# A two-layer hybrid trunk on one core: the build's scheduler with another simulated machine

## The chip, the cores and the metric

One Trainium2 chip, one of its cores. The metric is the device time of one execution in microseconds (us). The kernel is built with the Tile layer of the Bass language: the Python program traces instructions, a scheduler in the build orders them, and the result is one fixed instruction stream for each engine.

## The reference

The reference computes two layers of a diffusion trunk over 1024 latent tokens and a prompt of 128 tokens, 1024 channels wide, in 32-bit floats. Each layer is

```python
h = rms_norm(x, P['g_pre_mix']) * (1.0 + sc1) + sh1
o, extra = mixer(h)
x = x + gt1 * rms_norm(o, P['g_post_mix'])
h = rms_norm(x, P['g_pre_mlp']) * (1.0 + sc2) + sh2
m = einsum(square(relu(einsum(h, P['mlp_w1']))), P['mlp_w2'])
x = x + gt2 * rms_norm(m, P['g_post_mlp'])
```

where the scales, shifts and gates come from a conditioning vector times `w_ada`. The mixer is one input projection (`w_in`) that feeds four groups of heads: latent attention (MLA), banded attention with a sink (SWA), a gated delta rule that runs forward and backward over the tokens in chunks of 64 (GDN), and a long convolution of order 2 (Hyena). Their outputs are concatenated and multiplied by `w_out`. Beside the two token streams the kernel returns the prompt's keys, values and final GDN states.

## The kernel before

`Trunk.build` traces two layers one after the other. All 1152 tokens (9 tiles of 128) are handled together. Each wide product is split in two halves of precision: an operand x becomes `hi` (rounded) and `lo` (the rest, made at L232), and `mm3` (L215 to L219) multiplies hi by hi, hi by lo and lo by hi. So a weight tile is loaded by DMA into a staging buffer of the pool `T`, which has 4 buffers (L251 in `load_cols`, L241 in `load_rows`), cast on ScalarE (ACT) and subtracted on VectorE (DVE) before TensorE (PE) can use it.

A layer has these stages, in the order of the trace:

- the normed and transposed input, and 22 tiles of the input projection (`pj`), traced by a generator `rest` (L2098) that goes on to the Hyena convolutions and the six attention heads;
- beside it a generator `other` (L2108) with the GDN: two preparations (`gdn_prep`, L1083) and a scan of 16 serial steps (`gdn_scan`), all of it traced with a priority raised by 300 (L2121);
- a third generator `adas` (L2092) that loads `w_ada` in 192 pieces of 256 KB in all and multiplies them (`ada`, L385 to L396);
- the output projection (`out_proj`, L1744) with the second norm;
- the MLP (`mlp`, L1776): 15 blocks and a last one (`mlp_last`), each with two column tiles of `w1` (hidden, PSUM tiles `hid`) and two row tiles of `w2` (output, PSUM tiles `mo`), summed into SBUF tiles `acc`.

`run_timed` (L2190) weaves the three generators by hand-given weights, so the trace order is already an interleaving. All DMAs, loads and stores alike, are issued by one engine, SyncE (SP), in one queue. In a few places `issue_after` pins a DMA behind another one on SP.

One place matters below. In `gdn_prep` a 32 by 32 triangular inverse `N` is built in 31 serial steps, for the forward direction on DVE and for the backward direction on GpSimd (POOL) (L1195 to L1204). Then, for each direction, ACT makes a transposed copy `Tb` and SP stores both:

```python
for dr in range(2):
    Tb = W("Tb", (32, 32))
    nc.scalar.copy(out=Tb[:72], in_=N[dr][:72]...)      # L1209
    nc.sync.dma_start(out=nscr[dr, 0]..., in_=N[dr]...)  # L1210
    nc.sync.dma_start(out=nscr[dr, 1]..., in_=Tb...)     # L1211
```

They are read back in another layout (`NT` L1221, `NaTG` L1224), and the products `G` follow on PE. The other place is the attention's row of maxima: ACT writes `mrow` (L719), SP stores it (L720) and reads it back.

What the scheduler does with the trace, by the library's own description: each engine has a heap of instructions by priority, which is the place in the traced program (with the raise above). It runs a simulated machine; when an engine is free there, the instruction of the highest priority whose inputs are finished and whose tile has a free slot in its pool is taken next. The order in which instructions are taken is the order of the engine's stream on the chip, and the slot that was free is the buffer. Waits on semaphores are then added for what the streams need of one another. [...] `TileContext` at L2229 has a flag for which simulated machine is used.

## Time and profile before

| | us |
|---|---|
| median of 3 runs | 3828.64 |
| fastest and slowest of them | 3820.32 and 3840.5 |
| the profiled execution | 3820.2 |
| its span, first to last instruction | 3818.4 |
| TensorE busy in it | 3535.5 |
[...]

The times are of whole executions. The rows below come from the profiled one, whose own time is 8.4 us under the median and 1.8 us over its span. Busy time of PE is the union of its matmuls; a stretch that runs at the lower clock counts as busy for longer. In a timeline the number in brackets is how long the engine sat idle before the instruction, and what released it.

### The profile page before, as it was taken

The page shows a single profiled execution, that of the slowest core. Times are in us where ns is not written, and L with a number is a line of the kernel's source. Part 1 is how long each engine was busy: PE and PEld are TensorE (multiplying, and loading weights), DVE is VectorE, ACT ScalarE, POOL GpSimd, SP SyncE. Part 2 cuts the span into 40 slices and gives each one's busy share as a digit, 9 for nine tenths or more (in the row PEclk, how much of TensorE's full clock was granted, in tenths as well). Part 3 has the DMA queues.
Part 4 walks back from the last instruction along what each step waited for, and adds up shares of the span by engine and source line. Part 5 has one row for each costly group of instructions (what it writes and reads, how often), then busy time and mean ns, then how long its engine had stood idle before and what let it go on. Part 6 is the DMA issues. An engine that isn't in the chain of part 4 may idle for free. (4 is left out here: it accounts for less than half of the span.)

```text
span 3818.4 us, 57318 instructions
## 1 busy us (share of the span) xinstructions
PE 3535.5 (93%) x21674; PEld 2988.0 (78%) x21674; DVE 2278.2 (60%) x4583; ACT 1349.5 (35%) x2930; POOL 857.7 (22%) x806
## 2 busy tenths in 40 slices
PE   7989888799999999999989888877999999999998
PEld 4879774376789999999878887545767899999997
DVE  5765567697645444444586673677884544444446
ACT  5434343265543112212364334323554422222112
POOL 1152531164420000000131642213553200000003
PEclk9999889897999999999999898896889999999999
DMA  5346476832421111111324455765314211111113
GB/s 203 115 118 159 135 261 205 242 80 59 148 80 50 39 45 45 41 37 45 109 100 137 121 138 164 251 208 139 96 40 139 72 45 45 44 45 45 39 39 121
DMA packets 364670, 405.29 MB, mean 106 GB/s; under 512 B 115815, under 2 KB 237157, under 8 KB 364394
## 3 DMA queue, kind: packets, MB, share of 16 engines
q1 hardware_dynamic: 364394, 401.63, 34.2%
q8 instruction: 170, 2.79, 0.3%
q14 instruction: 106, 0.87, 0.1%
HBM read 298.34 MB, written 103.19 MB: 105 GB/s over the span
## 5 line engine op out<-in xcount | busy, mean ns | idle before, releaser
L213 PE MATMUL hid<-hT,w1h 128*128 128x384 f32 x3072 | 786.6, 335 | 0.1
L213 PE MATMUL pj<-hT,wah 128*128 128x384 f32 x2112 | 574.4, 350 | 8.9 <-ACT hu L1740 3.9
L1823 DVE TENSOR_TENSOR acc<-acc,mo 128x512 f32<-128x512 f32 x504 | 345.9, 686 | 391.9 <-PE mo L213 391.9
L213 PEld LDWEIGHTS hid<-hT,w1h 128*128 128x128 f32 x3072 | 557.7, 188 | 14.4 <-ACT h L481 1.1
L213 PE MATMUL hid<-hT,w1l 128*128 128x384 f32 x1536 | 514.2, 335 | 0.0
L213 PE MATMUL mo<-w2h,ul 128*128 128x512 f32 x1116 | 435.2, 392 | 0.0
L213 PE MATMUL mo<-w2h,uh 128*128 128x512 f32 x1080 | 422.8, 391 | 0.0
L213 PE MATMUL mo<-w2l,uh 128*128 128x512 f32 x1080 | 422.6, 391 | 0.0
L213 PEld LDWEIGHTS pj<-hT,wah 128*128 128x128 f32 x2112 | 395.0, 196 | 21.9 <-issue 6.0
L662 POOL TENSOR_TENSOR e<-e,e 128x512 f32<-128x512 f32 (+1 forms) x216 | 312.9, 1450 | 298.0 <-ACT e L651 141.6
L269 POOL TENSOR_TENSOR postr<-postr,mhalf 128x1 f32<-128x1 f32 x36 | 22.4, 623 | 1570.4 <-DVE postr L268 1569.1
L213 PE MATMUL pj<-hT,wal 128*128 128x384 f32 x1056 | 367.2, 348 | 0.0
L242 ACT CAST w2h<-w 128x512 fp32r<-128x512 f32 x128 | 70.3, 619 | 732.9 <-PE mo L213 728.8
L213 PEld LDWEIGHTS hid<-hT,w1l 128*128 128x128 f32 x1536 | 288.2, 188 | 2.5
L232 DVE TENSOR_TENSOR el<-e,eh 128x512 fp32r<-128x512 f32 (+1 forms) x252 | 252.4, 1023 | 33.8 <-ACT eh L653 31.9
L213 PEld LDWEIGHTS mo<-w2h,ul 128*128 128x128 f32 x1116 | 209.7, 188 | 46.2
L213 PEld LDWEIGHTS mo<-w2h,uh 128*128 128x128 f32 x1080 | 202.8, 188 | 37.5
L213 PEld LDWEIGHTS mo<-w2l,uh 128*128 128x128 f32 x1080 | 202.7, 188 | 36.5
L213 PEld LDWEIGHTS pj<-hT,wal 128*128 128x128 f32 x1056 | 205.8, 195 | 3.7 <-issue 2.0
L1806 DVE SCALAR_TENSOR_TENSOR relu<-hid,relu 128x384 f32<-128x384 f32 x180 | 99.4, 553 | 166.8 <-ACT relu L1805 166.8
L213 PE MATMUL ada<-wada,cst 128*32 128x512 f32 x384 | 138.2, 683 | 31.3 <-DMA wada<-in_w_ada 31.0
L1805 ACT ACTIVATE relu<-hid 128x384 f32<-128x384 f32 x180 | 87.9, 488 | 184.4 <-PE hid L213 184.4
(498 smaller groups left out, 6360.2 us busy)
## 6 DMA issues: line engine op xcount, KB each, us to landing
w<-in_w SPq DMA_DIRECT2D x256, 256.0 KB
wada<-in_w_ada SPq DMA_DIRECT2D x192, 256.0 KB
wa<-in_wa SPq DMA_DIRECT2D x88, 256.0 KB
x<-xres SPq DMA_DIRECT2D x21, 512.0 KB
x<-in_x SPq DMA_DIRECT2D x18, 512.0 KB
Q<-rscr SPq DMA_DIRECT2D x32, 288.0 KB
o<-oscr SPq DMA_DIRECT2D x18, 512.0 KB
xres<-x SPq DMA_DIRECT2D x36, 256.0 KB
```

The lines of the kernel that those rows point to most:

```text
L213: self.last = self.nc.tensor.matmul(out, l, r, start=start, stop=stop, skip_group_check=True)
L232: self.nc.vector.tensor_tensor(out=lo, in0=x, in1=hi.bitcast(F32), op=ALU.subtract)
L242: self.nc.scalar.copy(out=hi[:, q], in_=st)
L269: self.nc.gpsimd.tensor_tensor(out=out, in0=out, in1=self.bcs(self.mhalf[:out.shape[0]], out.shape), op=ALU.pow)
L662: self.nc.gpsimd.tensor_tensor(out=acc, in0=acc, in1=e, op=ALU.add)
L1805: nc.scalar.activation(out=r[:, :n], in_=ps[:, :n], func=AF.Relu)
L1806: nc.vector.scalar_tensor_tensor(out=r[:, :n], in0=ps[:, :n], scalar=0.0, in1=r[:, :n], op0=ALU.max, op1=ALU.mult)
L1823: nc.vector.tensor_tensor(out=acc[t][:, ns], in0=acc[t][:, ns], in1=ps, op=ALU.add)
```

## The change

The build's scheduler gets its other simulated machine: it runs against the library's core simulator in place of its timeline simulator. The traced program, its priorities, the pools and the operations stay as they are; what can differ is each engine's order, the buffer that a tile gets, and the waits that follow from both.

```diff
-    with tile.TileContext(nc, schedule_with_timeline_sim=True) as tc:
+    with tile.TileContext(nc, schedule_with_timeline_sim=False) as tc:
         Trunk(tc, I, O).build()
```

## Rows read from the trace of the kernel before

**Rows 1.** The page's first lines: span, and PE's busy time and instructions.
```profile
span 3818.4 us, 57318 instructions
PE 3535.5 (93%) x21674; PEld 2988.0 (78%) x21674; DVE 2278.2 (60%) x4583; ACT 1349.5 (35%) x2930; POOL 857.7 (22%) x806
```
**Rows 2.** Stretches: start:end length, busy by engine (count), clock, DMA share, GB/s.
```profile
0.00:42.00 42.00, 29.20 (x96) 8.75 (x96) 18.68 (x39) 14.00 (x29) 2.92 (x8) 1.00 0.84 304
42.00:1000.00 958.00, 850.99 (x6249) 673.07 (x6247) 658.94 (x1511) 426.42 (x954) 349.90 (x326) 0.89 0.50 148
1000.00:1113.00 113.00, 110.18 (x512) 88.97 (x511) 51.46 (x104) 52.19 (x110) 32.10 (x34) 1.00 0.42 138
1113.00:1905.00 792.00, 791.84 (x4023) 720.96 (x4024) 394.96 (x649) 184.30 (x377) 25.85 (x25) 1.00 0.16 52
1905.00:1968.00 63.00, 46.62 (x249) 37.71 (x248) 49.23 (x97) 43.53 (x100) 31.68 (x29) 0.86 0.27 92
1968.00:2895.00 927.00, 802.98 (x6026) 649.23 (x6025) 652.93 (x1429) 397.67 (x890) 341.81 (x317) 0.88 0.47 141
2895.00:3038.00 143.00, 138.50 (x658) 113.96 (x658) 62.85 (x134) 59.40 (x129) 38.76 (x40) 1.00 0.34 116
3038.00:3806.00 768.00, 765.16 (x3873) 695.36 (x3871) 383.69 (x622) 172.00 (x348) 26.17 (x23) 1.00 0.16 52
3806.00:3818.40 12.40, 0.00 (x0) 0.00 (x0) 5.52 (x6) 0.00 (x0) 8.53 (x7) 0.54 0.34 128
```
**Rows 3.** The same view, three stretches inside the second layer's mixer.
```profile
1968.00:2200.00 232.00, 214.44 (x1728) 197.20 (x1728) 153.55 (x332) 97.79 (x181) 74.02 (x82) 0.95 0.45 133
2200.00:2422.00 222.00, 186.01 (x1983) 174.19 (x1982) 134.65 (x326) 89.07 (x231) 73.90 (x89) 0.91 0.54 155
2422.00:2605.00 183.00, 143.54 (x1173) 82.48 (x1172) 135.21 (x411) 51.55 (x170) 37.13 (x38) 0.84 0.73 235
```
**Rows 4.** Timeline of PE, 262 to 300 us: start, length, instruction [idle before].
```profile
265.41 1.14 PE L229 MATMUL ht<-ident,hc 128*128 128x128 f32 x9
284.85 0.70 PE L213 MATMUL G<-NaTG,Q 32*32 32x32 f32 x8 [18.30 <-DMA NaTG<-nscr]
285.48 1.01 PE L213 MATMUL pj<-hT,wah 128*128 128x384 f32 x2
...
293.77 0.33 PE L213 MATMUL pj<-hT,wal 128*128 128x384 f32 x1
```
**Rows 5.** Timeline of ACT, 262 to 292 us.
```profile
281.38 1.95 ACT L1209 COPY Tb<-N 72x1024 f32<-72x1024 f32 x1 [15.39 <-POOL N L1204]
283.23 0.61 ACT L253 CAST wah<-wa 128x512 fp32r<-128x512 f32 x1
283.75 0.47 ACT L518 COPY hcx<-pj 128x384 f32<-128x384 f32 x1
```
**Rows 6.** Timeline of POOL, 262 to 284 us: the last step of N.
```profile
281.08 0.27 POOL L1204 TENSOR_TENSOR N<-N,tmp 72x31 f32<-72x31 f32 x1
```
**Rows 7.** Timeline of SP's DMA issues, 255 to 300 us.
```profile
264.65 0.31 SPq L1211 DMA_DIRECT2D nscr<-Tb  x1
281.37 0.29 SPq L1210 DMA_DIRECT2D nscr<-N  x1
...
291.38 1.18 SPq L251 DMA_DIRECT2D wa<-in_wa  x2
```
**Rows 8.** Waits of PE over the whole span: us in total, times, longest.
```profile
PE ada L213 <- DMA wada<-in_w_ada: 31.0, 24, 5.9
PE G L213 <- DMA NaTG<-nscr: 31.0, 9, 18.3
...
PE ST L213 <- DMA Q<-mscr: 9.9, 1, 9.9
```
**Rows 9.** Waits of SP's DMA queue over the whole span, same columns.
```profile
SPq L251 <- DVE w2l L232: 784.3, 59, 27.3
...
SPq L720 <- ACT mrow L719: 178.1, 14, 40.3
```

## The prediction, as it was put on record

> **What bounds the kernel now.** I read the page's head first: TensorE is busy for 3535.5 of 3818.4 us, 93%, and no other engine is over 60% [rows 1]. That would say "TensorE-bound, nothing to win or lose by order", but it is an average, so I cut the span into stages [rows 2]. The reader is to see two kinds. The two MLP stretches (1113 to 1905 and 3038 to 3806) are 1560 us long and TensorE is busy in 1557.0 of them, at the full clock of 2.4 GHz. The two output projections (113 and 143 us) have 248.7 of 256 busy. The mixers and the passage between the layers (42 to 1000, 1905 to 1968, 1968 to 2895) are 1948 us long, and there TensorE is busy for 851.0 + 46.6 + 803.0 = 1700.6 us, 87.3%, at a mean granted clock of 0.86 to 0.89, which means that it spends part of that time at the lower level of 1.2 GHz. 247.4 us of idle TensorE lie in these stretches, against 3 us in the MLP. Start and end (42 and 12.4 us) complete the span.
>
> So the change can act on about half of the span. What ends the idle stretches there is read from TensorE's waits: they are many and small, spread over some 60 pairs of waiter and releaser; the largest two sums are 31.0 us each [rows 8]. There is no single stall whose removal or growth is the answer; the question is how well four streams of work (projection and attention, GDN, Hyena, conditioning) fill one another's gaps.
>
> **What one misjudged place costs.** The longest wait of all, 18.3 us, shows what an order can do [rows 4 to 7]. POOL finishes the last step of the backward inverse N at 281.3. ACT's stream has the copy `Tb`, which needs this N, ahead of the cast of the next projection weight and ahead of the copy that empties a projection's PSUM tile, so ACT sits idle for 15.4 us and those two run at 283.2 and 283.8. SP's stream has the store of the same N ahead of the next weight loads, so between 265.0 and 281.4 it issues nothing, and the weights are issued at 291.4. TensorE, whose projection needs the weight and the PSUM tile, and whose `G` needs N, sits from 266.5 to 284.9. When it starts again, two matmuls take 1.01 us together, where the same pair took 0.51 before the gap, until the clock is back some 6 us later. The simulated machine let the copy go first because in its time N was ready; on the chip it was not. One such error, in two queues at once, costs 18.3 us of idle and about 3 us of slow matmuls.
>
> **The change part by part.** There is one edit with three effects.
>
> (1) Removed and added work: none. The same matmuls, copies and DMAs are issued. Cost 0; TensorE's busy time at the full clock can't change.
>
> (2) The MLP and the output projections: the order there follows from buffers and data. SP spends 784.3 us in 59 waits, about 13 us each, for staging or weight buffers to come free [rows 9], so the loads run ahead of TensorE as far as the buffers go under any order that respects the trace. I take 0. What covers it is one block of matmuls, 1560/32 = 49 us for each of the 32 blocks; were the cover gone and each block paid one load wait like the longest single one of an attention tile, 9.9 us [rows 8], it would be 317 us. With 3 us of idle time in 1560 nothing can be gained there.
>
> (3) The mixers: every engine's order is drawn again, from other durations and other landing times. The trace of before shows neither, so I bound it by stretches of the kernel that show the same kind of work at a better and a worse fill [rows 3]. If all 1700.6 us of busy time were filled as 1968 to 2200 is (214.44/232 = 92.4%), the mixers would take 1840 us, 108 less. If all were filled as 2422 to 2605 is (143.54/183 = 78.4%), they would take 2168, 220 more. Filled as the GDN preparation beside the projection of the second layer (2200 to 2422, 186.01/222 = 83.8%): 2030, which is 82 more. As a scale for what one order differs from another: the first layer's mixer has 851.0/958 = 88.8% and the second's 803.0/927 = 86.6%, with nearly the same work; over 1948 us these two shares are 49 us apart.
>
> I take the middle one, +82 us, nearest to the row of 2200 to 2422. The reason is where the idle time comes from. It is made where an in-order queue holds an instruction whose input comes later than the simulation had it (the 18.3 us above). A machine that follows queues, contention and durations less closely has more of these, and 82 us are four places of 18.3 + 3 us more, in two layers with two GDN preparations, two convolutions and six heads each. An order that by luck removes the present ones gains at most their sum. The row against me is the same one: the present machine, too, misjudged POOL, so it isn't exact either.
>
> Sum: 3820.2 (the profiled execution) + 0 + 0 + 82 = 3902; the median of the runs is 8.4 us above that execution, so 3910.
>
> **A rule weighed.** The row: from 266.5 to 284.9 TensorE sat still with projection matmuls behind `G` in its stream, and `G` went first when it came [rows 4]. [...]
>
> **The rivals.**
>
> *Faster.* The new order no longer puts the backward `Tb` and its store ahead of weights in ACT's and SP's streams. Place: the four GDN preparations. For it: the 31.0 us that TensorE waits for `NaTG` [rows 8], 18.3 of them in one wait, are errors of the present order; the work to fill them was there. Price: with the `NaTG` waits and as much again from the conditioning loads (31.0) gone, 62 us, so 3767 from the median; at most the 108 us of the bound, 3720. It decides from the point where POOL's last step is simulated to end after the projection's next weight is ready. Against it: these are 62 of 247 us, and the other 185 us are drawn again too.
>
> *No change.* Data dependences and few buffers (4 staging buffers) fix the order so far that both machines come to nearly the same streams; or the flag has no effect. 3829, within 19. For it: the MLP is such a case. Against it: in the mixers four streams with work ready at the same time compete for each queue.
>
> *Much slower.* SP stops at a store while loads that TensorE needs stand behind it. Place: the attention's store of `mrow`: SP already sits 178.1 us in 14 waits for it, up to 40.3 each, and only 9.9 us of that reaches TensorE [rows 8, 9], because what stands behind is not needed yet. Price with this cover gone: 168 us more, 3997. It decides from the point where a load needed within 40 us is queued behind such a store.
>
> **How the numbers follow.** A difference of 0.5%, 19 us, is about what a measurement of this kernel can tell from none. Chances: the forecast (slower by 20 to 150 us) 0.51, much slower (150 to 260) 0.18, no change 0.13, faster 0.18. Faster 0.18, same 0.13, slower 0.69. The range: the upper end is the bound of 220 us, 4040 from the profiled execution, above which I leave a third of the much slower case, 0.06. The lower end is 3780, which leaves the better part of the faster case, 0.10. That is 0.16 outside. The forecast's own range is 3848 to 3979.
>
> **What would show it.** In the profile after: TensorE still 99% busy or more in both MLP stretches, so that they keep 1560 us (if not, step 2 is wrong); TensorE's idle time in the mixers about 330 us in place of 247 and their clock at or under 0.88 (step 3); new waits of 5 us or more of TensorE on a load or on ACT, with SP or ACT idle before a store or copy that needs POOL, DVE or ACT (the mechanism). If the idle time grows without such long waits, spread over many small ones, the size may be right and the mechanism is wrong. If the wait for `NaTG` goes and nothing takes its place, the faster rival holds. If the streams are the same, nothing changes.

## The result, and the profile after

| | before | after |
|---|---|---|
| median of 4 runs each, taken side by side, us | 3826.47 | 4146.99 |
| ratio of the times, 95% interval | | 1.083 [1.081, 1.086] |
| the profiled execution, us | 3820.2 | 4145.76 |
| TensorE busy in it, us | 3535.5 | 3753.4 |
| mean granted clock of TensorE | 0.941 | 0.902 |

The change makes the kernel 8.3% slower. The forecast was 3910 with a range of 3780 to 4040: the direction was right, and the time lies 107 us above the range.

The page's first lines of after (answers to [rows 1]):

```profile
span 4144.0 us, 57252 instructions
PE 3753.4 (91%) x21674; PEld 3091.4 (75%) x21674; DVE 2314.4 (56%) x4583; ACT 1360.2 (33%) x2930; POOL 837.0 (20%) x806
```

The instructions are the same, 21674 matmuls in both. The reader is to see that the busy time of TensorE grew by 217.9 us with equal matmuls, and its idle time (span less busy) by 107.7, from 282.9 to 390.6. The sum is the 325.6 us that the span grew.

Not all of the added busy time comes from the clock. The traces tell the granted clock at every moment: TensorE is busy at the full clock (1.00) for 3209.9 us in before and 3117.9 in after, and at the lower level, half of it (0.50), for 325.6 and 635.5. If work takes twice as long at half the clock, an estimate from the pair of matmuls that the prediction names (1.01 us right behind the 18.3 us gap, at 0.50, against 0.51 before it, at 1.00; the next pairs at 0.50 take 0.84), the clock accounts for half of the 309.9 us more, 155 us; the other 63 of the 217.9 us are busy time that it does not explain by this estimate.

Where they lie. I cut both spans at the same events of TensorE: the first and last matmul of the input projection `pj`, the first transpose `hoT` of the convolutions' output (the attention takes over), the first matmul of the output projection, the first of the MLP.

| stage, us | layer 0 before | after | layer 1 before | after |
|---|---|---|---|---|
| up to the projection | 42.0 | 56.5 | | |
| projection, with GDN preparation | 495.8 | 572.9 | 490.8 | 611.8 |
| convolutions | 161.1 | 170.3 | 175.7 | 169.5 |
| attention | 303.1 | 371.1 | 288.7 | 336.2 |
| output projection | 111.7 | 105.7 | 116.7 | 114.9 |
| MLP, to the next projection or the end | 817.3 | 815.7 | 815.5 | 819.4 |

Projection (+198) and attention (+116) hold nearly all of it; another 14.5 us lie ahead of the first projection. The same cuts as stretches of the trace (start:end length, then busy time and count of PE, PEld, DVE, ACT and POOL, PE's clock, DMA share, GB/s), before:

```profile
42.00:538.00 496.00, 441.07 (x3840) 404.03 (x3838) 308.54 (x738) 220.23 (x478) 161.42 (x183) 0.91 0.49 141
538.00:699.00 161.00, 130.29 (x1211) 75.59 (x1209) 123.32 (x385) 49.05 (x172) 34.21 (x37) 0.87 0.76 243
699.00:1002.00 303.00, 281.20 (x1207) 194.10 (x1205) 228.38 (x392) 158.69 (x306) 156.19 (x108) 0.87 0.40 108
1931.00:2422.00 491.00, 428.81 (x3869) 395.06 (x3869) 312.16 (x703) 209.02 (x461) 161.83 (x183) 0.92 0.48 139
2422.00:2597.00 175.00, 137.56 (x1144) 76.89 (x1143) 128.31 (x387) 49.04 (x165) 37.13 (x38) 0.85 0.73 236
2597.00:2886.00 289.00, 255.97 (x1139) 193.90 (x1139) 230.75 (x376) 158.46 (x307) 156.65 (x108) 0.84 0.30 80
```

and after (the last two are the MLPs):

```profile
56.00:629.00 573.00, 497.28 (x4649) 438.73 (x4650) 343.76 (x907) 251.70 (x615) 156.82 (x179) 0.89 0.41 121
629.00:800.00 171.00, 116.20 (x403) 59.74 (x402) 107.09 (x235) 9.25 (x13) 36.58 (x38) 0.80 0.73 235
800.00:1171.00 371.00, 339.34 (x1214) 220.30 (x1213) 235.33 (x366) 163.63 (x311) 149.06 (x108) 0.78 0.28 76
2092.00:2704.00 612.00, 531.27 (x4669) 459.41 (x4670) 347.98 (x893) 258.10 (x624) 165.42 (x187) 0.84 0.41 119
2704.00:2873.00 169.00, 109.82 (x397) 58.69 (x396) 105.35 (x234) 9.58 (x18) 36.37 (x37) 0.82 0.72 230
2873.00:3210.00 337.00, 309.82 (x1150) 215.07 (x1149) 228.39 (x363) 162.59 (x310) 150.05 (x108) 0.78 0.23 60
...
1276.00:2068.00 792.00, 785.54 (x3993) 715.70 (x3993) 398.54 (x652) 188.30 (x382) 28.05 (x28) 1.00 0.16 52
...
3324.00:4092.00 768.00, 767.28 (x3913) 699.81 (x3914) 381.16 (x618) 175.15 (x348) 15.85 (x16) 1.00 0.15 48
```

Three things are to be seen. About 800 matmuls moved from the convolutions (1211 to 403) into the projection (3840 to 4649), and the convolutions did not get shorter for it (some 20 us of each are now one wait, named below). The attention has the same matmuls (1207 and 1214) and is 93% busy before and 91% after, yet it takes 68 us longer, at a clock of 0.78 in place of 0.87. The MLPs are as they were.

The moved matmuls are the GDN scan's. The matmuls that write or read a tile `u` of the scan, in the first two stretches of layer 0, before:

```profile
42.00:538.00 496.00, 11.00 (x320) 8.80 (x320) 8.87 (x52) 9.23 (x34) 0.91 0.49 141
538.00:699.00 161.00, 26.85 (x832) 21.47 (x832) 30.62 (x164) 30.32 (x110) 0.87 0.76 243
```

and after:

```profile
56.00:629.00 573.00, 51.53 (x1152) 38.54 (x1152) 39.26 (x216) 37.15 (x144) 0.89 0.41 121
629.00:800.00 171.00, 0.00 (x0) 0.00 (x0) 0.00 (x0) 0.00 (x0) 0.80 0.73 235
```

All 1152 run inside the projection now, where 832 ran beside the convolutions.

The waits that the prediction's mechanism is about (us in total, times, longest; answers to [rows 8, 9]). TensorE's of after:

```profile
PE G L213 <- DMA NaTG<-nscr: 33.3, 9, 18.7
PE O L213 <- DVE el L232: 27.6, 63, 2.1
PE pj L213 <- ACT wah L253: 26.9, 4, 13.2
...
PE oT L229 <- DVE gsk L276: 20.7, 1, 20.7
PE oT L229 <- DVE gsr L277: 19.9, 1, 19.9
```

SP's, after and then before:

```profile
SPq L1210 <- POOL N L1204: 87.8, 4, 27.3
```

```profile
SPq L1210 <- POOL N L1204: 18.3, 2, 16.3
```

ACT's, after and then before:

```profile
ACT e L651 <- PE ST L213: 197.7, 86, 37.2
```

```profile
ACT e L651 <- PE ST L213: 68.1, 38, 16.2
```

SP stands before POOL's `N` in all four GDN preparations now, 87.8 us against 18.3, but TensorE's wait for `NaTG` is about what it was (31.0). The two longest waits of after are new: once in each layer, in the convolutions, TensorE stands some 20 us before the transposes `oT` of the scan's output. The wait for the cast weight `wah` has no counterpart in before either. In all, TensorE idles for 5 us or longer 10 times in before (85.7 us) and 16 times in after (153.1 us), which is 67.4 of the 107.7 us of idle time added. In the attention ACT's exponentials `e` wait for the scores tile `ST` three times as long.

### The profile page after: what moved, and what is told of

Read it like the earlier page. It is cut to its first block, busy times and chain, and to the rows that moved or that the text cites. A ratio compares the mean times of both kernels' runs of the same rounds, so it can differ in the third digit from the quotient of the medians.

```text
span 4144.0 us, 57252 instructions
## 1 busy us (share of the span) xinstructions
PE 3753.4 (91%) x21674; PEld 3091.4 (75%) x21674; DVE 2314.4 (56%) x4583; ACT 1360.2 (33%) x2930; POOL 837.0 (20%) x806
## 3 DMA queue, kind: packets, MB, share of 16 engines
q1 hardware_dynamic: 364394, 401.63, 31.4%
## 5 line engine op out<-in xcount | busy, mean ns | idle before, releaser
L213 PE MATMUL pj<-hT,wah 128*128 128x384 f32 x2112 | 598.3, 360 | 37.7 <-ACT wah L253 26.9
L662 POOL TENSOR_TENSOR e<-e,e 128x512 f32<-128x512 f32 (+1 forms) x216 | 299.1, 1385 | 493.1 <-ACT e L651 315.0
L213 PE MATMUL pj<-hT,wal 128*128 128x384 f32 x1056 | 380.4, 361 | 6.7 <-DVE wal L232 6.7
L269 POOL TENSOR_TENSOR postr<-postr,mhalf 128x1 f32<-128x1 f32 x36 | 19.9, 554 | 1597.0 <-DVE postr L268 1589.8
L651 ACT ACTIVATE e<-ST 128x512 f32<-128x512 f32 x162 | 96.3, 597 | 237.9 <-PE ST L213 197.7
```

Of the source, the lines that this page charges most:

```text
L213: self.last = self.nc.tensor.matmul(out, l, r, start=start, stop=stop, skip_group_check=True)
L269: self.nc.gpsimd.tensor_tensor(out=out, in0=out, in1=self.bcs(self.mhalf[:out.shape[0]], out.shape), op=ALU.pow)
L651: nc.scalar.activation(out=e[:, :n], in_=ps[:, :n], func=AF.Exp, scale=scale)
L662: self.nc.gpsimd.tensor_tensor(out=acc, in0=acc, in1=e, op=ALU.add)
```

## Experiments

All kernels below are the same traced program unless a diff says otherwise. Most fix an engine's order with edges that add no wait: the program is built once with the other flag, its order is taken, and the second build must keep that order for chosen engines and for instructions traced in chosen stages. The diffs are shortened.

```diff
+def pinned(order, engines):
+    place = {n: k for k, n in enumerate(order)}
+    def pin(tc, line):
+        for e, stages in engines.items():
+            mine = [i for k, i in enumerate(line) if str(i.engine).endswith(e) and i.name in place and stage(k) in stages]
+            mine.sort(key=lambda i: place[i.name])
+            for a, b in zip(mine, mine[1:]):
+                tc.add_manual_dep(b, a.name, NoSync, reason="order of the other schedule")
...
-    with tile.TileContext(nc, schedule_with_timeline_sim=True) as tc:
+    with tile.TileContext(nc, schedule_with_timeline_sim=False) as tc:
         Trunk(tc, I, O).build()
+        pin(tc, nc.cur_bb.bb.instructions)
...
+    order_of_before = order_of(arrays, True)
```

"Front" is what is traced from the start of a layer's mixer (in the first layer from the start of the program) to its attention, "attention" what is traced from there to the output projection, "rest" the output projection and the MLP.

| run | build | pinned or edited | median, us | ratio to before, 95% |
|---|---|---|---|---|
| e1 | after | all engines to before's order | 3836 | 1.001 [0.998, 1.003] |
| e2 | after | TensorE | 4074 | 1.064 [1.060, 1.067] |
| e3 | after | front: all | 3986 | 1.040 [1.037, 1.044] |
| e4 | after | attention: all | 4061 | 1.061 [1.058, 1.064] |
| e5 | after | front: all; attention: TensorE | 3901 | 1.018 [1.014, 1.022] |
| e6 | after | front: all; attention: all but TensorE | 3969 | 1.035 [1.031, 1.040] |
| e7 | after | attention: all; front: SP | 4031 | 1.052 [1.048, 1.056] |
| e8 | after | attention: all; front: TensorE, SP | 3975 | 1.037 [1.033, 1.041] |
| e9 | after | scan traced late | 4092 | 1.070 [1.065, 1.074] |
| e10 | after | split scores tiles joined | 4140 | 1.082 [1.079, 1.086] |
| e11 | after | e9 and e10 | 4089 | 1.068 [1.064, 1.072] |
| e12 | after | `Tb` and `N` stores on POOL | 4139 | 1.082 [1.078, 1.085] |
| e13 | after | scores raised by 40 | 4118 | 1.074 [1.070, 1.079] |
| e14 | after | e9 and e13 | 4065 | 1.062 [1.057, 1.067] |
| e15 | before | attention: TensorE to after's order | 3967 | 1.035 [1.030, 1.039] |
| e16 | before | scores raised by 40 | 3863 | 1.008 [1.006, 1.011] |
| e17 | after | front: all; attention: scores and O on TensorE | 3913 | 1.022 [1.018, 1.026] |
| e18 | after | all engines to after's order, 168 matmuls more | 4131 | 1.078 [1.075, 1.081] |

### Is it the order alone?

```diff
+        pin = pinned(order_of_before, {e: ("front", "attention", "rest") for e in ("PE", "SP", "Activation", "DVE", "Pool")})
```

> The build of after, with every engine's instruction order pinned to the order of before (edges that fix only the order in a stream, no waits). What stays of after is what its simulated machine does beside the order: which free buffer a tile gets, and the waits that follow. Theory 'order alone': 3827 us, within 15 of before. Rival 'buffers': the buffers were handed out by a machine with other durations, so waits for slots stay; some 3900 or more.

Measured: 3836 us, ratio 1.001. The page's head:

```profile
span 3828.3 us, 57317 instructions
PE 3542.6 (93%) x21674; PEld 2993.3 (78%) x21674; DVE 2278.9 (60%) x4583; ACT 1353.0 (35%) x2930; POOL 856.6 (22%) x806
```

Busy and idle time of TensorE are back within 8 us. Order alone carries the loss; the buffers that the other machine hands out cost nothing that can be measured.

### Which stage

```diff
+        pin = pinned(order_of_before, {e: ("front",) for e in ("PE", "SP", "Activation", "DVE", "Pool")})
```

> The build of after with all engines pinned to before's order only for what is traced before a layer's attention (projection, GDN, Hyena convolutions, and the conditioning beside them). By the stage marks of the two traces the attention stages are longer by 72 + 47.5 = 120 us in after, the stages before them by about 205. Theory 'two separate losses': 4147 - 205 = 3942. Rival 'the attention only pays for the state in which the convolutions leave it' (work postponed into it): 3830 to 3860.

and with `("attention",)` in its place:

> The build of after with all engines pinned to before's order only for what is traced from the start of a layer's attention to its output projection. Theory 'two separate losses': the attention's 120 us go, 4027. Rival 'the attention only pays for what comes before it': 4120 to 4150, no gain.

Measured: 3986 and 4061. The front's order is worth 161 us, the attention's 86; together (4147 to 3829) they are worth 318, so 71 us are gone only when both are as before. My split by stages (205 and 120) was too simple. The attention stretches of e3 show why:

```profile
693.00:1101.00 408.00, 361.29 (x1234) 232.92 (x1232) 251.37 (x404) 166.04 (x313) 151.61 (x109) 0.73 0.30 81
...
2694.00:3055.00 361.00, 329.51 (x1168) 230.99 (x1169) 233.70 (x385) 163.27 (x309) 148.82 (x108) 0.72 0.25 66
```

With the front as fast as in before (the attention begins at 693), the other machine's attention takes 408 and 361 us, not 371 and 336. So the attention's order costs 105 and 72 us in that setting; a slow front hides some of it.

### Which engine's queue

```diff
+        pin = pinned(order_of_before, {"PE": ("front", "attention", "rest")})
```

> The build of after with only TensorE's order pinned to before's; SP, ACT, DVE and POOL keep what after's simulated machine gives them under that constraint. Theory 'TensorE's own stream' (the GDN scan drawn into the projection, the shifted-matmul groups of the attention split): most of the 320 us goes, 3830 to 3890. Rival 'the queues that feed it' (SP behind POOL's N store, ACT held by a copy): the waits stay and a fixed TensorE order can't step around them, 4050 to 4200.

Measured: 4074, only 73 us better than after. Waits of TensorE in it:

```profile
PE pj L213 <- DVE wal L232: 50.4, 4, 19.3
PE X L213 <- DVE ZA L1445: 49.3, 3, 22.6
```

Its busy time came down from 3753 to 3595, but its idle time rose from 391 to 480 (span 4075.8): a good order of TensorE fed by queues of another order stands and waits. The time lies in the range of the rival, that the queues that feed it hold the loss.

```diff
+        pin = pinned(order_of_before, {"PE": ("front", "attention"), "SP": ("front",), "Activation": ("front",), "DVE": ("front",), "Pool": ("front",)})
```

> The build of after; before the attention stages all engines are pinned to before's order (as in the third run, 3986 us), and in the attention stages TensorE alone is pinned too. Theory 'TensorE's own stream' (groups of three shifted matmuls split up, so that ACT gets its tile late): the 157 us that the attention still costs go, 3830 to 3870. Rival 'the queues around it' (ACT's order of exponentials, SP's stores): TensorE's order alone doesn't help, 3940 to 4000.

and with the attention for the other four engines in place of PE:

> As the run before, but in the attention stages SP, ACT, DVE and POOL are pinned to before's order and TensorE is left to after's machine. Theory 'TensorE's own stream': little is gained over 3986, some 3940 to 3990. Rival 'the queues around it': 3830 to 3870.

Measured: 3901 and 3969. In the attention TensorE's order is worth 85 of the 157 us that remained in e3, the other four queues together 17; the last 55 or so need both.

```diff
+        pin = pinned(order_of_before, {"SP": ("front", "attention"), "PE": ("attention",), "Activation": ("attention",), "DVE": ("attention",), "Pool": ("attention",)})
```

> The build of after; attention pinned on all engines to before's order (as in the fourth run, 4061 us), and before the attention SP alone is pinned too. Theory 'SP stands behind the stores of POOL's N': in after these waits are 87.8 us against 18.3, so about 70 us go, 3990. Rival 'TensorE's stream, which takes the GDN scan early and leaves the convolutions alone': SP's order changes little, 4040 to 4070.

and with the front for PE too:

> The build of after; attention pinned on all engines, and before it TensorE and SP are both pinned to before's order; ACT, DVE and POOL are left to after's machine. Theory 'TensorE's stream and SP's carry the loss': 3830 to 3860. Rival 'the in-order queues of ACT and DVE, which copy and cast what the projection needs, carry a part of their own': 3900 or more.

Measured: 4031 and 3975, from 4061. In the front SP is worth 31 us, SP and TensorE 86; the other 146 are gone only when ACT, DVE and POOL have before's order too. SP alone gave 31 of the 70 us expected, and in the second run the rival held, that ACT's and DVE's queues carry a part of their own. In e8 the mechanism of the prediction can be read in the open, between 40 and 800 us, in the waits of TensorE and of ACT:

```profile
PE G L213 <- DMA NaTG<-nscr: 32.4, 2, 31.4
```

```profile
ACT Tb L1209 <- POOL tmp L1202: 28.0, 1, 28.0
ACT Tb L1209 <- DVE N L1204: 22.8, 1, 22.8
```

ACT stands at the copy `Tb` for 28.0 and 22.8 us, and TensorE, in before's order, waits 31.4 us for `NaTG` in one piece.

### Two places by themselves, and the prediction's mechanism

```diff
-            yield from until("z")
+            yield from until("proj")
+            self.done.add("scan")
             yield from self.gdn_scan(l, self.gdn_tag)
...
-                with self.tc.high_priority(300):
+                with contextlib.nullcontext() if "scan" in self.done else self.tc.high_priority(300):
                     t = next(g, "end")
```

> The build of after with one edit in the traced program: the GDN scan is traced after the projection and without the raised priority, so that in TensorE's stream 369 and 376 of its 432 u matmuls of the two layers stand behind the last projection matmul (before: 312 and 288; after: none). Nothing is pinned. Theory 'the scan's place': in after the projection stages took 573 and 612 us against 496 and 491, and the convolutions, now alone, 171 and 169 against 161 and 175. With the scan beside the convolutions again the projections go back to some 515 each and the convolutions stay near 175: 4147 - 150 = 4000, between 3960 and 4030. Rival 'the queues that feed the projection': 4100 or more.

Measured: 4092, 55 us better, where 150 were expected. By stretches, layer 0 (projection, convolutions, attention):

```profile
56.00:556.00 500.00, 430.70 (x3655) 398.40 (x3654) 295.57 (x677) 200.89 (x424) 151.49 (x176) 0.91 0.43 124
556.00:753.00 197.00, 145.18 (x1374) 86.11 (x1373) 140.41 (x424) 58.85 (x202) 38.38 (x40) 0.81 0.67 216
753.00:1159.00 406.00, 361.17 (x1235) 230.06 (x1234) 251.99 (x404) 166.02 (x313) 151.63 (x109) 0.74 0.30 81
```

The projection came down from 573 to 500 us as foreseen (layer 1: 612 to 522). But 27 us of that went into the convolutions and 35 into the attention, which is as slow here as in e3. In both layers together the two projections gave back 162 us, of which the convolutions took 53 and the attentions 54. That the scan's place lengthens the projection is shown; that moving it back wins the time is shown for a third of it.

```diff
+def joined(order):
+    follows = {n for g in GROUPS for n in g[1:]}
+    first = {g[0]: g for g in GROUPS}
+    return [m for n in order if n not in follows for m in first.get(n, [n])]
...
+        pin = pinned(joined(order_of_after), {"PE": ("attention",)})
```

> The build of after; in the attention stages TensorE keeps after's own order except that the three matmuls of each scores tile ST stand together again where the first one stood (in after 110 of 162 tiles are split up by other matmuls, in before none). The other engines are ordered by after's machine around that. Theory 'the split': ACT gets each scores tile earlier and the 85 us go that TensorE's whole attention order was worth (3986 to 3901): 4062, between 4040 and 4085. Rival 'other parts of the order of attention': 4120 to 4150.

Measured: 4140, no change that can be told from after (1.082 against 1.083). The split, which I had read off the trace as the cause in the attention, is not it by itself.

Both diffs together:

> Both edits of the two runs before in the build of after. If the scan's place and the split are two separate losses with these prices: 4147 - 147 - 85 = 3915. If the first only shifts work into the attention, near 4000; if neither matters, over 4100.

Measured: 4089, which is e9 again.

```diff
-            nc.scalar.copy(out=Tb[:72], in_=N[dr][:72]...)
-            nc.sync.dma_start(out=nscr[dr, 0]..., in_=N[dr]...)
-            nc.sync.dma_start(out=nscr[dr, 1]..., in_=Tb...)
+            nc.gpsimd.tensor_copy(out=Tb[:72], in_=N[dr][:72]...)
+            nc.gpsimd.dma_start(out=nscr[dr, 0]..., in_=N[dr]...)
+            nc.gpsimd.dma_start(out=nscr[dr, 1]..., in_=Tb...)
```

> The build of after with the copy Tb and the four stores of N and Tb of a GDN preparation put on POOL and its own DMA queue, behind POOL's N, so that neither ACT nor SP stands before N. This is the prediction's mechanism by itself. Theory 'a queue that stands before POOL's N costs the time': SP's 87.8 us of waiting there go and the 33.3 us that TensorE waits for NaTG shrink, 4060 to 4110. Rival 'those waits are covered by other work': 4130 to 4150, or some us more for the slower copy.

Measured: 4139, not to be told from after either. TensorE still waits for `NaTG`:

```profile
PE G L213 <- DMA NaTG<-nscr: 35.3, 7, 18.8
```

SP's waits at the store of `N` are gone (it stands longer for staging buffers now, 113.8 us at `wal` in place of 52.4), and nothing that can be measured is won: the products `G` need `N` itself, whoever stores it. The mechanism on which the prediction was built is real (e8), and at this place it costs nothing that can be measured in after. Other places of it, the waits at `oT` and `wah` above, no run takes away.

### What it is in the attention's order

In TensorE's stream I counted, for each of the 252 score tiles, how many other score tiles are completed between it and the product `O` that needs its exponentials: 3.34 on average in before, 1.61 in after.

```diff
                 ps = self.P(name="ST")
-                self.mm_shift(ps, k, q)
+                with self.tc.high_priority(40):
+                    self.mm_shift(ps, k, q)
```

Likewise the scores `sT`, the exponential, `eh` and `el`.

> The build of after with the scores matmuls of the attention and the chain behind them (exponential, cast eh, rest el) traced at a priority raised by 40, nothing pinned. In TensorE's stream there are then 3.02 other scores tiles between a scores tile and its O (after 1.61, before 3.34). Theory 'distance': the 85 us that TensorE's attention order was worth go, and as ACT and DVE are drawn to match up to 120: 4030 to 4062. Rival 'the attention is slow for another reason (its order of sS, sC, rb, den; the clock it starts with)': 4120 or more, as with the joined tiles.

Together with the diff of e9:

> The same raise together with the late scan (that alone 4092). In the late-scan run the projections had come down to 500 and 522 us but the attentions had grown to 405 and 355. If distance is what the attention lacks, it goes to some 310 to 330 there: 4092 - 100 = 3990. If it isn't, 4070 to 4095.

Measured: 4118 and 4065, 29 and 27 us better than without the raise (4147 and 4092), where 85 to 105 were expected. That is about a third of what TensorE's order is worth there; the intervals of e9 and e14 overlap a little. The raise also draws the exponentials and casts of ACT and DVE forward, so that the distance itself wins this third is not shown.

```diff
     with tile.TileContext(nc, schedule_with_timeline_sim=True) as tc:
         Trunk(tc, I, O).build()
+        pin = pinned(order_of_after, {"PE": ("attention",)})
```

> The reverse: the build of before, where in the attention stages TensorE alone is pinned to after's order (distance 1.61, 110 scores tiles split), and the other engines are drawn by before's machine around it. Theory 'distance': 85 to 157 us slower than before, 3915 to 3985. Rival 'the attention only suffers from what came before it in after': 3829 to 3850.

Measured: 3967, 140 us slower than before, as expected. Its attention stretches:

```profile
698.00:1086.00 388.00, 342.68 (x1204) 218.70 (x1204) 249.31 (x392) 165.51 (x307) 152.68 (x109) 0.75 0.31 85
2674.00:3031.00 357.00, 319.99 (x1136) 221.75 (x1135) 242.60 (x388) 163.33 (x305) 148.38 (x108) 0.73 0.26 67
```

This is the cleanest run of the study: the good machine, the same matmuls, and only TensorE's order of the attention prescribed (the other engines are drawn by before's machine around it). The stage grows by 85 and 68 us, of which TensorE's busy time is 61.5 and 64.0 (342.68 and 319.99 against 281.20 and 255.97), and the clock falls from 0.87 and 0.84 to 0.75 and 0.73. The two profiled spans are 147 us apart; by the estimate from the two levels 107 of them are the clock, 17 other busy time and 23 idle time.

The diff of e13 in the build of before:

> The build of before with the raise by 40. Its distance goes only from 3.34 to 3.43, so by the theory of distance it stays where it is, 3829 within 20. If it is faster, before's attention lacked something that the mean distance doesn't show.

Measured: 3863, 36 us slower than before with the same mean distance (3.43). The theory of distance had 3829 within 20, so the mean distance isn't the measure of a good order, and the raise makes no better kernel.

```diff
-            ... if stage(k) in stages
+            ... if stage(k) in stages or stage(k) == "attention" and e == "PE" and i.name in CHAIN
```

Here `CHAIN` holds the matmuls of ST, sT, O and sO, and the stages are the front's, of all engines.

> As the run with before's order pinned ahead of the attention (3986 us), and in the attention only the scores (ST, sT) and the products O and sO keep before's order among themselves on TensorE; the matmuls that prepare the next head (S, sS, sC), the sums and divisions (den, rb) and all other engines are left to after's machine. Theory 'scores against products': all that TensorE's whole order gave, 3901, within 20. Rival 'the matmuls beside them': 3950 to 3990.

Measured: 3913, 73 of the 85 us of e5. What counts in TensorE's order is how scores and products follow each other; the matmuls of the next head's preparation, the sums and the divisions leave 12 us, and the intervals of e5 and e17 overlap. Which feature of that sequence it is, beyond the distance, stays open.

### Lost slots or a lost clock?

```diff
         self.mm(out, k[0][:97], q[0][:97], True, False)
+        self.mm(out, k[0][:97], q[0][:97], True, False)
         self.mm(out, k[0][:96], q[1][:96], False, False)
```

All engines are pinned to `order_of_after`, each repeated matmul right behind its first.

> The build of after with every engine pinned to its own order (that of after), plus 168 repeated matmuls: the first of the three of each scores tile is issued twice, into the same PSUM tile, which changes no result. At 0.39 us each at the full clock they are 66 us of work, at the mean of after's attention (0.49 us) 82. If TensorE is bound by its matmuls there: 4147 + 66 to 82 = 4213 to 4229. If they fall into the 59 us of idle time of the two attention stages: 4150 to 4180. If the clock falls because TensorE is too little loaded and the additional load keeps it up: below 4147, as far as 4080.

Measured: 4131, 16 us less than after by the medians; the intervals of the two ratios, [1.075, 1.081] and [1.081, 1.086], just don't meet. The 66 us that were expected of the added matmuls are their lengths added up, and matmuls overlap (in the first MLP stretch of after one starts every 198 ns, and one of `hid` lasts 334): in busy time, with a microsecond at the lower level counted as half, they add 37. Even so the kernel isn't slower. Its attention stretches:

```profile
793.00:1155.00 362.00, 336.50 (x1299) 225.24 (x1297) 232.10 (x367) 163.94 (x311) 149.19 (x108) 0.84 0.29 78
2855.00:3187.00 332.00, 309.79 (x1232) 221.02 (x1231) 225.85 (x362) 163.56 (x311) 149.53 (x108) 0.82 0.23 61
```

85 and 82 matmuls more than in after's rows above, busy for 2.8 us less in layer 0 and the same in layer 1, because the clock stands at 0.84 and 0.82 in place of 0.78. So more matmuls alone kept the clock higher there, and much of the added busy time of after's attention is a lost clock: by the estimate from the two levels, 80 of the 112 us in the two stages. The other 32 are not the clock. No run pins after's order without the added matmuls, so the pinning itself is taken to cost nothing, as in e1.

## Why the prediction was wrong

**Step 1, work removed and added.** Right as to the count: 21674 matmuls in both. The sentence that "TensorE's busy time at the full clock can't change" doesn't hold by the traces: with a microsecond at the lower level counted as half, it rose from 3372.7 to 3435.6 us. In e9, with the scan late, it is 3390.2, so most of this goes with the scan's place. The sentence was also used for more than it says, in step 3.

**Step 2, MLP and output projections.** Right. The two MLPs went from 817.3 to 815.7 and from 815.5 to 819.4 us, 99% and 100% busy at the full clock (1.00 in both stretches); the output projections were 6 and 2 us shorter. What the two levels are in GHz no run shows: the traces give them as 1.00 and 0.50 of the full clock, and no number of the sum rests on GHz.

**Step 3, the mixers.** Here the sum failed. It held TensorE's 1700.6 us of busy time constant and let only the fill change, for 82 us. The fill was sized well: the idle time in the six stretches shown of projection, convolutions and attention went from 240 to 329 us (the forecast said "about 330 in place of 247"), over the whole span by 107.7. The term that was left out is the busy time itself, 217.9 us. 3820.2 + 217.9 + 107.7 = 4145.8, the profiled execution. The clock is the larger part of that term, 155 us by the estimate above, and 63 us are not the clock. A matmul of the form 96 by 512 for the scores took 421 ns on average in before's first attention and 481 in after's. One of the scan added 33 ns of busy time in before (76.07 us for 2304 in both layers) and 51 in after (118.55). That isn't the clock alone: with the lower level counted as half, the 76.07 and 118.55 us are 70.5 and 97.2.

The rows to see it by were there. In [rows 3] the clock goes with the fill: 0.95 at 92.4%, 0.91 at 83.8%, 0.84 at 78.4%. The working took the fill of these stretches and not their clock, and the clock that it named as a sign, 0.88 or under, is about that of before; the 18.3 us gap was priced with 3 us of slow matmuls after it [rows 4]. With fill times clock the worst stretch gives 0.784 * 0.84 = 0.659 against 0.873 * 0.884 = 0.772 of the mixers now, and 1948 * 0.772 / 0.659 - 1948 = 334 us in place of 220. That end would have held the result, but this is hindsight: the middle row (0.838 * 0.91 = 0.763), which the prediction chose, would have given only 23 us.

The matmuls' busy share gives no measure of the loss here: in the first attention it went from 93% to 91% while the stage took 22% longer. The share of the weight loads moved a little more, from 64% (194.10 of 303) to 59% (220.30 of 371), and gives the size no better.

**The mechanism.** A queue that stands before an instruction whose input comes late exists (ACT before `Tb` for 28.0 us in e8), and SP's waits before `N` grew as foreseen, from 18.3 to 87.8 us. But at `N` it is not where the time went: taking it away (e12) changed nothing that can be measured (4139 against 4147). Long waits did come at other places, as the signs asked (at `wah` on ACT, up to 13.2 us) or nearly so (at `oT` on DVE, 20.7 and 19.9). Waits of 5 us or longer are most of the added idle time, and what they cost the kernel is not shown. Idle time is a third of the loss. Most of the time went into two stages whose change the prediction hadn't named: the projection, into which the GDN scan was drawn forward from the convolutions, where TensorE is idle for 31 us of 161 in before; and the attention, where scores and products stand closer together. In the attention TensorE's order alone brings the clock down (e15, from 0.87 and 0.84 to 0.75 and 0.73) and more matmuls bring it up (e18, from 0.78 to 0.84 and 0.82). In the projection the clock fell too, from 0.91 and 0.92 to 0.89 and 0.84, but no run tests what brought it down there.

**The order in TensorE's stream.** That the order of instructions matters is borne out: order alone explains all of it (e1, 3836 us from 4147), and 140 us hang on TensorE's order in the two attentions (e15). That matmuls never pass one another in the queue isn't shown by this.

**The rivals.** Faster: the `NaTG` waits stayed (31.0 to 33.3). No change: no. Much slower: the price of 3997 came nearest, but not by its mechanism; SP's wait for `mrow` fell from 178.1 to 160.9 us, and TensorE's wait for the row that comes back (9.9 us, [rows 8]) has no successor among its larger waits.

**What stays open.** What the two simulated machines have different can't be read from a trace. In the front 146 of 232 us belong to ACT's, DVE's and POOL's order once SP and TensorE are fixed, and no single place was found for them. In the attention the sequence of scores and products is the carrier (e17), and raising the scores, which brings the mean distance near before's, wins about a third. In the projections and convolutions 68 of the 117 us of added busy time are the clock by the estimate from the two levels; no run separates them there.

## What to carry to other kernels

When an order gets worse, price the clock with the fill: take both from the same stretch, and multiply. That gives a bound, not a forecast (334 us from one row here, 23 from another). Look for stages that hold work of TensorE at little cost (here the convolutions, 161 us with 1211 matmuls and 170 with 403, though 197 with 1374 in e9): work that leaves them for a fuller stage is paid there, in the projections 162 us by e9. An order is one thing across all engines: half of a good order, pinned onto the other half of a bad one, won 73 us of 320 (e2).

## What the runs showed of the hardware

TensorE ran for long at the lower clock with hardly a gap. Three stretches of after's first attention:

```profile
1024.00:1036.00 12.00, 12.00 (x29) 7.50 (x27) 6.28 (x13) 5.29 (x9) 4.24 (x4) 0.50 0.00 0
...
1060.00:1072.00 12.00, 11.61 (x50) 7.27 (x48) 9.21 (x17) 5.65 (x12) 5.92 (x5) 0.92 0.10 23
1072.00:1084.00 12.00, 11.60 (x31) 7.53 (x32) 7.62 (x20) 4.68 (x13) 4.71 (x4) 0.50 0.01 2
```

In the first TensorE is busy for all of 12.00 us, and its granted clock is 0.50 throughout; the last is 97% busy, right behind a stretch at 0.92. Its last idle gap of more than 1 us before these stretches ends at 984.64, and none of more than 0.7 us follows before 1100:

```profile
984.64 0.50 PE L213 MATMUL O<-el,VA 128*128 128x512 f32 x1 [1.59 <-DVE el L232]
```

So a high busy share and the absence of long gaps did not keep the clock up there. The busy share doesn't tell how closely matmuls follow: they overlap, and in the first MLP stretch of after one starts every 198 ns (3993 in 792 us) while one of `hid` lasts 334 ns. And in e18 more matmuls in the same order raised the clock, from 0.78 to 0.84 and 0.82, and the kernel took no longer with them.
